# A hybrid diffusion step on one core: up projection in products of 388, 384 and 386 columns, head maxima in two float32r products, transposing mode, a shorter layer-norm sum, and stores moved between queues

## The chip, the core and the metric

The kernel runs on 1 core of one Trainium2 chip. The metric is the device time of one execution in microseconds (us). TensorE does the matrix products into PSUM (8 banks), VectorE and ScalarE do elementwise work, GpSimd and SyncE mainly issue transfers here. Each engine works through its own instructions in order; semaphores join them.

## What is computed

One layer of a diffusion backbone for 128 context tokens and 256 latent tokens (384 in all), width 2048, in float32:

```python
h = rmsnorm(x, norm_mix_pre) * (1 + sc1) + sh1
z = h @ w_in + b_in
glu = z[..., :WA] * sigmoid(z[..., WA:2*WA])
a = along_rows(dwconv(31 taps), glu)
y_a = silu(layernorm(a, ln_a_w, ln_a_b)) @ w_a_out          # layer norm over 512 channels
y_b = einsum(pool_groups(...), w_pool) * pool_scale
hc, new_state = mlstm_bidir(q, k, v, gates, C0, n0, m0)     # 4 heads of 256, two directions
y_c = (hc * rsqrt(mean(hc * hc) + EPS) * mlstm_norm_w * sigmoid(og)) @ w_c_out
mix = (ga * y_a + gb * y_b + gc * y_c) @ w_out
x = x + g1 * rmsnorm(mix, norm_mix_post)
h2 = rmsnorm(x, norm_ffn_pre) * (1 + sc2) + sh2
u, g = split(h2 @ w_ffn_up, 2)                              # 2048 -> 2 x 5632
f = (gelu(dwconv(g, 3 taps)) * u) @ w_ffn_down
x = x + g2 * rmsnorm(f, norm_ffn_post)
```

The mLSTM weights scores by `exp(logd - m_t)`, where `m_t` is a running maximum per head and direction.

## The kernel before

Activations lie transposed, features on the 128 partitions and the 384 tokens along the free dimension, in 16 blocks `hx[k]`. Every float32 operand of a large product is split in two float32r parts: `hi`, a rounded copy by ScalarE, and `lo`, the rest, by VectorE (`split`, L167). A product is then three products into the same PSUM bank (`mm3`, L176): `wh x hi`, `wh x lo`, `wl x hi`, recorded as L177, L178 and L179. In the value projection they are L877 to L879, in the down projection L1490 to L1492.

The weights come as a stream of pieces of 512 KB (24 products each where a tile of 128 output features takes 8 blocks). `run_stream` (L187) writes the order of all engines by hand: for each piece it splits the piece two ahead, issues the piece's products, then the work that evacuates the piece before, and then one entry of each of three background queues `bgq`. Three buffers each hold split weights, so a split waits until TensorE has left the piece three back.

The parts that the change touches:

- Gates and heads. `gate_rows3` (L621) writes the negated running maxima `NM` (36 rows x 512 columns). For each head `head_parts` queues 14 steps; step `s1` multiplies `NM` by a column of the identity repeated 128 times, so that one head's row stands on all partitions (L913, float32), adds the masks (L916), computes the scores, and turns K by two products with the identity (L928). Step `s12` turns the head's output by six products with the identity (L1034), after `s11` has scaled it on VectorE (L1022).
- Layer norm of the convolution branch, `ln_parts` (L707): its 9 steps stand in a background queue beside the heads' steps. `p1` and `p3` sum the four channel tiles, and their squares, over the partitions by four products each with a matrix of ones (L713, L727), in banks 4 to 7 that the heads use too.
- Up projection. The scale of the RMS norm is applied after the product, so the two shift vectors (context and latent) ride along as two extra columns of `hx[k]`: 386 columns instead of 384. `h2_step` (L1309) makes block k+2 while TensorE works on block k of the first six tiles (`up0_use`); the other 82 tiles follow in `up_use`. `up_after` evacuates a pair of tiles.
- End. `down_last` (L1529) finishes the three token blocks of the second half of the output one after another; `down_out` takes the squares (ScalarE, L1524) and evacuates (VectorE, L1526); `down_finish` (L1546) scales four column blocks (VectorE, L1553) and stores each.

Two transpositions elsewhere already use TensorE's transposing mode: the residual, turned by 48 of them (L1451).

```python
            if t:
                down_finish(t - 1)
        down_finish(2)
```

## Time and profile before

| | |
|---|---|
| median of 3 runs | 2293.03 us (2292.72 to 2294.73) |
| the profiled execution | 2294.96 us |
| its span, first to last instruction | 2293.2 us |
| mean granted TensorE clock | 0.993 |
| TensorE busy | 2253.0 us (98%), 12597 products |
| VectorE busy | 1426.8 us (62%) |
| ScalarE busy | 880.8 us (38%) |
| GpSimd busy | 31.7 us (1%) |
| DMA | 390.05 MB, mean 170 GB/s |

The profiled execution's own time is 1.8 us more than its span; what lies around the span is start and end of the program. A busy time adds up durations that overlap in TensorE's pipeline, so a product's price is better read from the distance between the starts of two products than from its duration.

### The profile page before, as it was taken

Reading aid. Unit: us, or ns where it says so; the run is one execution under the profiler, and the core shown is the slowest. Engines: PE = TensorE matmul, PEld = TensorE weight load, DVE = VectorE, ACT = ScalarE, POOL = GpSimd, SP = SyncE. Lnnn points to the kernel's source line nnn. Section 1 sums busy time; section 2 is a strip of 40 time slices with the busy share of each in tenths; the row PEclk is TensorE's granted clock in tenths of the full one; section 3 lists DMA queues with packets and bytes.
Section 4 is the critical chain, followed back from the end, with each engine's and each line's share of the span. In section 5 each row is a group of like instructions: output and inputs, shape, how many; then the busy total and the mean of one; then the engine's idle time right before and its main releaser. Section 6 shows DMA issues by size and latency. Waiting matters only on the chain.

```text
span 2293.2 us, 31786 instructions
## 1 busy us (share of the span) xinstructions
PE 2253.0 (98%) x12597; PEld 2143.6 (93%) x12597; DVE 1426.8 (62%) x2230; ACT 880.8 (38%) x1362; POOL 31.7 (1%) x72
## 2 busy tenths in 40 slices
PE   6999999999999999999999999999999999999997
PEld 3799999999999999999989999999999999888886
DVE  3466777655888888868476577775444445444445
ACT  3443333534232322343366433333333334334332
POOL 0000000000000000000000000000000000000000
PEclk8999999999999999999999999999999999999999
DMA  9944333325666676667433455554433333334342
GB/s 397 392 140 122 122 107 118 120 94 180 221 221 224 232 230 222 223 226 274 146 99 127 135 185 192 180 189 151 140 127 126 122 127 123 131 129 150 129 131 101
DMA packets 104869, 390.05 MB, mean 170 GB/s; under 512 B 12112, under 2 KB 12256, under 8 KB 100624
## 3 DMA queue, kind: packets, MB, share of 16 engines
q1 hardware_dynamic: 99504, 371.76, 47.9%
q0 software_dynamic: 4064, 14.36, 1.9%
q8 instruction: 98, 1.61, 0.3%
q10 hardware_dynamic: 1152, 1.90, 0.2%
q14 instruction: 51, 0.42, 0.1%
HBM read 382.71 MB, written 5.27 MB: 169 GB/s over the span
## 4 chain that ended last, share of the span: by engine, by line
PE 97%; DVE 1%; DMA 1%; ACT 1%; issue 0%; ACTq 0%; DVEq 0%
PE ps L177 24%; PE ps L179 24%; PE ps L178 24%; PE ps L1491 5%; PE ps L1490 5%; PE ps L1492 5%; PE ps L393 1%; PE ps L878 1%; PE ps L879 1%; PE ps L877 1%; DMA eraw<-w_ada 1%; PE ps L974 1%; PE ps L969 1%; PE ps L913 0%; DVE wlo L169 0%; DMA vec<-vec 0%
## 5 line engine op out<-in xcount | busy, mean ns | idle before, releaser
L169 DVE TENSOR_TENSOR wlo<-raw,whi 128x1024 fp32r<-128x1024 f32 (+3 forms) x521 | 622.2, 1197 | 726.9 <-ACT whi L168 724.7
L177 PE MATMUL ps<-hx,whi 128*128 128x384 f32 (+1 forms) x3024 | 1024.8, 339 | 5.6 <-ACT hx L1294 3.2
L179 PE MATMUL ps<-hx,wlo 128*128 128x384 f32 (+1 forms) x3024 | 1019.1, 337 | 0.8 <-DVE wlo L169 0.8
L178 PE MATMUL ps<-hx,whi 128*128 128x384 f32 (+1 forms) x3024 | 1018.9, 337 | 0.2 <-DVE hx L169 0.2
L168 ACT ACTIVATE whi<-raw 128x1024 fp32r<-128x1024 f32 (+3 forms) x521 | 540.0, 1038 | 1231.8 <-PE ps L178 748.2
L177 PEld LDWEIGHTS ps<-hx,whi 128*128 128x128 f32 x3024 | 570.4, 189 | 12.3 <-issue 5.0
L179 PEld LDWEIGHTS ps<-hx,wlo 128*128 128x128 f32 x3024 | 570.1, 189 | 2.0 <-DVE wlo L169 2.0
L178 PEld LDWEIGHTS ps<-hx,whi 128*128 128x128 f32 x3024 | 570.2, 189 | 1.2 <-DVE hx L169 0.5
L1155 DVE SCALAR_TENSOR_TENSOR cb<-raw,cb 128x1024 f32<-128x1024 f32 x256 | 313.0, 1223 | 7.3 <-DMA raw<-w_ada 1.3
L1491 PE MATMUL ps<-whi,hx 128*128 128x512 f32 x528 | 205.5, 389 | 0.8 <-DVE hx L169 0.8
L1490 PE MATMUL ps<-whi,hx 128*128 128x512 f32 x528 | 205.5, 389 | 0.0
L1492 PE MATMUL ps<-wlo,hx 128*128 128x512 f32 x528 | 205.4, 389 | 0.0
L1491 PEld LDWEIGHTS ps<-whi,hx 128*128 128x128 f32 x528 | 99.1, 188 | 21.7 <-DVE hx L169 1.1
L1490 PEld LDWEIGHTS ps<-whi,hx 128*128 128x128 f32 x528 | 99.1, 188 | 20.8 <-ACT hx L168 0.4
L1492 PEld LDWEIGHTS ps<-wlo,hx 128*128 128x128 f32 x528 | 99.1, 188 | 20.7
L692 DVE SCALAR_TENSOR_TENSOR cacc<-cbuf,vec,cacc 128x444 f32<-128x444 f32 x116 | 78.7, 678 | 2.8
L1382 DVE SCALAR_TENSOR_TENSOR t<-t,vec,t 128x192 f32<-128x192 f32 (+1 forms) x176 | 63.7, 383 | 16.0 <-ACT t L1373 12.8
L877 PE MATMUL ps<-whi,hx 128*128 128x256 f32 x192 | 56.5, 294 | 0.0
L878 PE MATMUL ps<-whi,hx 128*128 128x256 f32 x192 | 54.3, 283 | 0.0
L879 PE MATMUL ps<-wlo,hx 128*128 128x256 f32 x192 | 54.3, 283 | 0.0
L393 PE MATMUL ps<-eraw,cs 128*32 128x512 f32 x256 | 34.7, 675 | 18.6 <-DMA eraw<-w_ada 18.6
L169 DVE TENSOR_TENSOR hx<-f,hx 128x384 fp32r<-128x384 f32 x88 | 48.3, 550 | 0.0
(283 smaller groups left out, 1430.6 us busy)
## 6 DMA issues: line engine op xcount, KB each, us to landing
raw<-w_up SPq DMA_DIRECT2D x164, 512.0 KB, 3.6
raw<-w_in SPq DMA_DIRECT2D x163, 512.0 KB, 3.8
raw<-w_ada SPq DMA_DIRECT2D x128, 512.0 KB, 4.3
raw<-w_down SPq DMA_DIRECT2D x88, 512.0 KB, 3.3
eraw<-w_ada SPq DMA_DIRECT2D x32, 1024.0 KB, 17.1
raw<-w_out SPq DMA_DIRECT2D x32, 512.0 KB, 4.3
raw<-w_v SPq DMA_DIRECT2D x16, 512.0 KB, 4.0
raw<-w_br SPq DMA_DIRECT2D x16, 512.0 KB, 4.7
```

Of the source, the lines that this page charges most:

```text
L168: act.activation(hi, src, AF.Copy)
L169: dve.tensor_sub(lo, src, hi.bitcast(F32))
L177: pe.matmul(out, wh, x, start=first, stop=False, skip_group_check=True)
L178: pe.matmul(out, wh, xl, start=False, stop=False, skip_group_check=True)
L179: pe.matmul(out, wl, x, start=False, stop=last, skip_group_check=True)
L692: dve.scalar_tensor_tensor(a, b[:, j : j + CPOS], w, a, ALU.mult, ALU.add)
L877: pe.matmul(outs[t], xh, hi[:, a], start=k == 0 and t != 1, stop=False, skip_group_check=True)
L878: pe.matmul(outs[t], xl, hi[:, a], start=False, stop=False, skip_group_check=True)
L1155: dve.scalar_tensor_tensor(MX["junk"], raw, 1.0, MX["cb"][c][half], ALU.mult, ALU.mult, accum_out=MODR[:, m, n, c, half : half + 1])
L1490: pe.matmul(ps, xh, hi[:, w], start=first, stop=False, skip_group_check=True)
L1491: pe.matmul(ps, xl, hi[:, w], start=False, stop=False, skip_group_check=True)
L1492: pe.matmul(ps, xh, lo[:, w], start=False, stop=last, skip_group_check=True)
```

## The change

In the up projection the shift columns' high and low parts stand side by side in one operand `full`: the first product of a triplet takes 388 columns (tokens, shifts high, shifts low), the second the low part of the tokens alone (384), the third 386. The two sums of shift columns are added later, by VectorE, in `up_after`. The maxima `NM` are split in two float32r parts and multiplied in two products by a float32r copy of 40 columns of the identity, `identr`, which ScalarE makes at the start. K and the head's output are turned in transposing mode. The layer norm adds its four tiles on VectorE and sums by one product each; the second sum's bank is taken from the four banks that the z tiles rotate through, and the steps become 11. `down_finish(t)` is called for each token block right after its products, and all stores go to SyncE's queue but two of the last block. The scratch memory for the descriptors of GpSimd's transfers is halved.

```diff
-HW = NT + 2
+HW = NT + 4
...
+    identr = cp.tile([P, 40], F32R, name="identr")
...
+    act.activation(identr, ident[:, 0:40], AF.Copy)
...
     def gate_rows3():
-        NM = Z["p"].tile([36, 512], F32, name="NM")
         M = Z["M"]
-        gp.memset(NM, 0.0)
-        dve.tensor_scalar_mul(NM[:, 0:LAT], M[:, SEQ:], -1.0)
...
+        NM.hi = Z["p"].tile([36, 512], F32R, name="NMh")
+        NM.lo = Z["p"].tile([36, 512], F32R, name="NMl")
+        gp.memset(NM.hi.bitcast(F32), 0.0)
+        gp.memset(NM.lo.bitcast(F32), 0.0)
...
+            act.activation(NM.hi[rows, dst], M[rows, src], AF.Copy, scale=-1.0)
+            dve.scalar_tensor_tensor(NM.lo[rows, dst], M[rows, src], -1.0, NM.hi[rows, dst].bitcast(F32), ALU.mult,
+                                     ALU.subtract)
...
         def p1():
+            t = tmp()
+            dve.tensor_add(t, glu["d", 0], glu["d", 1])
+            for c in (2, 3):
+                dve.tensor_add(t, t, glu["d", c])
+            L["s"] = t
+
+        def p1b():
             L["ps"] = bgbank()
-            for c in range(4):
-                pe.matmul(L["ps"][:, :NT], ones, glu["d", c], start=c == 0, stop=c == 3)
+            pe.matmul(L["ps"][:, :NT], ones, L["s"], start=True, stop=True)
...
         def p3():
-            L["sq"] = []
-            L["ps"] = bgbank()
+            s = tmp()
             for c in range(4):
-                t = tmp()
-                act.activation(t, glu["d", c], AF.Square)
-                pe.matmul(L["ps"][:, :NT], ones, t, start=c == 0, stop=c == 3)
+                sumsq_tile(s, glu["d", c], c == 0)
+            L["sq"] = s
+
+        def p3b():
+            L["ps"] = accbank()
+            pe.matmul(L["ps"][:, :NT], ones, L["sq"], start=True, stop=True)
...
-        return [p1, p2, p3, p4, p5(0), p5(1), p5(2), p5(3), p5(4)]
+        return [p1, p1b, p2, p3, p3b, p4, p5(0), p5(1), p5(2), p5(3), p5(4)]
...
-                pe.matmul(ps, ident[0:36, r : r + 1].broadcast_to([36, P]), Z["NM"], start=True, stop=False,
-                          skip_group_check=True)
+                one = identr[0:36, r : r + 1].broadcast_to([36, P])
+                pe.matmul(ps, one, Z["NM"].hi, start=True, stop=False, skip_group_check=True)
+                pe.matmul(ps, one, Z["NM"].lo, start=False, stop=False, skip_group_check=True)
...
-                pe.matmul(psy[:, SEQ + c * P : SEQ + (c + 1) * P], k[c][:, 0:SEQ], ident, start=False, stop=True,
-                          skip_group_check=True)
+                pe.transpose(psy[:, SEQ + c * P : SEQ + (c + 1) * P], k[c][:, 0:SEQ], ident)
...
-                    pe.matmul(ps[:, t * P : (t + 1) * P], W["hs"][:, t, c * P : (c + 1) * P], ident, start=t == 0,
-                              stop=True, skip_group_check=True)
+                    pe.transpose(ps[:, t * P : (t + 1) * P], W["hs"][:, t, c * P : (c + 1) * P], ident)
...
     def h2_c(k):
         if k < KD:
-            dve.tensor_sub(hx[k].lo, HU[k], hx[k].hi.bitcast(F32))
+            h = hx[k]
+            h.lo = h.lo[:, :NT]
+            dve.tensor_sub(h.lo, HU[k][:, :NT], h.full[:, :NT].bitcast(F32))
+            dve.tensor_sub(h.full[:, NT + 2 :], HU[k][:, NT:], h.full[:, NT : NT + 2].bitcast(F32))
...
+    def up_mm(ps, wh, wl, x, first, last):
+
+        pe.matmul(ps[:, :HW], wh, x.full, start=first, stop=False, skip_group_check=True)
+        pe.matmul(ps[:, :NT], wh, x.lo, start=False, stop=False, skip_group_check=True)
+        pe.matmul(ps[:, : NT + 2], wl, x.full[:, : NT + 2], start=False, stop=last, skip_group_check=True)
...
-            act.activation(hb[:, 0:2], pu[:, NT:HW], AF.Copy)
-            act.activation(hb[:, 2:4], pg[:, NT:HW], AF.Copy)
+            hb4 = tmp("hb4", 8, bufs=2).rearrange("p (a c) -> p a c", a=2)
+            act.activation(hb4[:, 0], pu[:, NT:HW], AF.Copy)
+            act.activation(hb4[:, 1], pg[:, NT:HW], AF.Copy)
+            dve.tensor_add(hb.rearrange("p (a c) -> p a c", a=2), hb4[:, :, 0:2], hb4[:, :, 2:4])
...
-            if t:
-                down_finish(t - 1)
-        down_finish(2)
+            down_finish(t)
...
-            (sync if n % 2 else act).dma_start(o["y"][t * P : (t + 1) * P, n * NB : (n + 1) * NB], g)
+            (act if t == 2 and n % 2 else sync).dma_start(o["y"][t * P : (t + 1) * P, n * NB : (n + 1) * NB], g)
...
-    nc = bacc.Bacc("TRN2", target_bir_lowering=False, num_devices=1, dynamic_dma_scratch_size=8192)
+    nc = bacc.Bacc("TRN2", target_bir_lowering=False, num_devices=1, dynamic_dma_scratch_size=4096)
```

Where the code is written in another order, the engines' instructions move. First TensorE at the start of the first head (`s1`): before, the float32 product of the maxima of the first direction stands between the stream's products and the masks (`LDWEIGHTS` and `MATMUL` with `identb`).

```order
L179 MATMUL ps_1695<-hx_544,wlo_1621 128x384
L913 MATMUL ps_1727<-NM,ident 128x512
L916 LDWEIGHTS identb
L916 MATMUL ps_1727<-mask,identb 128x128
L916 LDWEIGHTS identb
```

And in the changed kernel:

```order
L180 MATMUL ps_1703<-hx_546,wlo_1629 128x384
L933 MATMUL ps_1735<-NMh,identr 128x512
L934 MATMUL ps_1735<-NMl,identr 128x512
L936 LDWEIGHTS identb
L936 MATMUL ps_1735<-mask,identb 128x128
```

One product has become two in the same place; nothing else in this piece moves, and the transpositions keep their places.

Second, VectorE where the layer norm meets the third head. Before, the layer norm's reciprocal (`sig<-t`) and the scaling of its tiles (`cout`) stand ahead of the head's last unit (`dn`, `hs`), with three weight splits (`wlo`) between them and the final scaling of the head's output (`hss`, L1020).

```order
L169 TENSOR_TENSOR wlo_3714<-raw_3480,whi_3713 128x1024
L733 RECIPROCAL sig_3745<-t_3743 128x384
...
L995 SCALAR_TENSOR_TENSOR hs_3372<-nd_3755,dn_3757,hs_3372 128x256
L169 TENSOR_TENSOR wlo_3763<-raw_3542,whi_3762 128x1024
L842 TENSOR_SCALAR k_3793<-ps_3662,vec 128x384
L745 TENSOR_TENSOR cout_1921<-cout_1921,t_3795 128x384
L169 TENSOR_TENSOR wlo_3814<-raw_3602,whi_3813 128x1024
L745 TENSOR_TENSOR cout_2453<-cout_2453,t_3843 128x384
L169 TENSOR_TENSOR yal_1066<-cout_1921,yah_1065 128x384
L1020 RECIPROCAL hss_3798<-hss_3798 128x3
L1022 TENSOR_SCALAR hs_3372<-hs_3372,hss_3798 128x256 x3
```

And in the changed kernel:

```order
L1014 SCALAR_TENSOR_TENSOR hs_3386<-nd_3756,dn_3758,hs_3386 128x256
L170 TENSOR_TENSOR wlo_3764<-raw_3556,whi_3763 128x1024
L861 TENSOR_SCALAR k_3794<-ps_3671,vec 128x384
L170 TENSOR_TENSOR wlo_3814<-raw_3615,whi_3813 128x1024
L752 RECIPROCAL sig_3845<-t_3843 128x384
L755 TENSOR_TENSOR cout_1931<-cout_1931,sig_3845 128x384
L756 TENSOR_SCALAR cout_1931<-cout_1931,vec 128x384
...
L756 TENSOR_SCALAR cout_3532<-cout_3532,vec 128x384
L1039 RECIPROCAL hss_3798<-hss_3798 128x3
L1041 TENSOR_SCALAR hs_3386<-hs_3386,hss_3798 128x256 x3
L170 TENSOR_TENSOR wlo_3873<-raw_3669,whi_3872 128x1024
```

The layer norm's reciprocal and its eight scalings now stand between the last weight split and the scaling of the head's output, which the transpositions of step `s12` read.

Third, VectorE at the end of the program. Before, the four scalings of token block 1 (`fo_18055` to `fo_19250`) stand behind both evacuations of block 2 (`fo_19274`, `fo_19290`).

```order
L1526 TENSOR_TENSOR fo_19274<-ps_18090,gb_18075 128x512
...
L1526 TENSOR_TENSOR fo_19290<-ps_18091,gb_18075 128x512
L1550 RECIPROCAL r_19292<-r_19292 128x1
L1553 SCALAR_TENSOR_TENSOR fo_18055<-fo_18055,r_19292,x_9047 128x512
...
L1553 SCALAR_TENSOR_TENSOR fo_19250<-fo_19250,r_19292,x_9047 128x512
L1550 RECIPROCAL r_19303<-r_19303 128x1
L1553 SCALAR_TENSOR_TENSOR fo_18069<-fo_18069,r_19303,x_9047 128x512
```

In the changed kernel they stand ahead of them (`fo_18176` to `fo_19382` is block 1, `fo_19406` and `fo_19422` block 2):

```order
L1578 RECIPROCAL r_19384<-r_19384 128x1
L1581 SCALAR_TENSOR_TENSOR fo_18176<-fo_18176,r_19384,x_9064 128x512
...
L1581 SCALAR_TENSOR_TENSOR fo_19382<-fo_19382,r_19384,x_9064 128x512
L1556 TENSOR_TENSOR fo_19406<-ps_18211,gb_18196 128x512
...
L1556 TENSOR_TENSOR fo_19422<-ps_18212,gb_18196 128x512
L1578 RECIPROCAL r_19424<-r_19424 128x1
L1581 SCALAR_TENSOR_TENSOR fo_18190<-fo_18190,r_19424,x_9064 128x512
```

Each block is scaled right behind its own evacuations. ScalarE's row of the end loses four of its six stores.

## Rows read from the trace of the kernel before

**Rows 1.** The page: the busy time of the engines (part 1), and the chain that ended last, by line (part 4).
```profile
PE 2253.0 (98%) x12597; PEld 2143.6 (93%) x12597; DVE 1426.8 (62%) x2230; ACT 880.8 (38%) x1362; POOL 31.7 (1%) x72
PE ps L177 24%; PE ps L179 24%; PE ps L178 24%; PE ps L1491 5%; PE ps L1490 5%; PE ps L1492 5%; PE ps L393 1%; PE ps L878 1%; PE ps L879 1%; PE ps L877 1%; DMA eraw<-w_ada 1%; PE ps L974 1%; PE ps L969 1%; PE ps L913 0%; DVE wlo L169 0%; DMA vec<-vec 0%
```

**Rows 2.** Busy time in stretches of the span: start and end, length, then busy us and instructions of TensorE, its weight loads, VectorE, ScalarE and GpSimd, the granted TensorE clock (1.00 is the upper level), the busy share of the DMA engines, GB/s. The heads, the restart ahead of the up projection, the up projection, the turning of the residual.
```profile
172.00:400.00 228.00, 228.00 (x1410) 218.94 (x1409) 167.75 (x306) 79.01 (x118) 7.50 (x17) 1.00 0.38 118
1156.00:1170.00 14.00, 9.06 (x39) 8.16 (x39) 7.85 (x15) 7.87 (x21) 0.00 (x0) 0.76 0.16 54
1228.00:1896.00 668.00, 668.00 (x3802) 667.79 (x3801) 397.29 (x623) 262.35 (x426) 1.60 (x3) 1.00 0.46 151
1270.00:1310.00 40.00, 40.00 (x247) 39.87 (x246) 20.54 (x32) 18.62 (x32) 0.00 (x0) 1.00 0.40 131
```

**Rows 3.** Timeline of TensorE: start us, duration us, engine, line, operation and its tiles, shape, count. First and 31st of a run of products with 384 columns, first and 31st of one with 386, first and 43rd of one with 512.
```profile
800.38 0.33 PE L177 MATMUL ps<-hch,whi 128*128 128x384 f32 x1
...
805.58 0.33 PE L177 MATMUL ps<-hx,whi 128*128 128x384 f32 x1
...
1500.08 0.34 PE L178 MATMUL ps<-hx,whi 128*128 128x386 f32 x1
...
1505.38 0.34 PE L178 MATMUL ps<-hx,whi 128*128 128x386 f32 x1
...
2271.50 0.39 PE L1492 MATMUL ps<-wlo,hx 128*128 128x512 f32 x1
...
2281.02 0.39 PE L1492 MATMUL ps<-wlo,hx 128*128 128x512 f32 x1
```

**Rows 4.** Timeline of TensorE at the start of the first head. Two float32 records make one float32 product.
```profile
200.12 0.34 PE L179 MATMUL ps<-hx,wlo 128*128 128x384 f32 x1
200.39 1.12 PE L913 MATMUL ps<-NM,ident 36*128 36x512 f32 x2
201.44 0.34 PE L916 MATMUL ps<-mask,identb 128*128 128x128 bf16 x3
...
205.17 0.61 PE L928 MATMUL ps<-ident,k 128*128 128x128 f32 x4
205.54 0.42 PE L177 MATMUL ps<-hx,whi 128*128 128x384 f32 x1
```

**Rows 5.** The chain that ended last, in order of time: start us, length us, what. A head's six products against the identity (12 records), and 12 transpositions of the residual (12 records).
```profile
265.02 1.34 PE ps L1034 x12
...
1275.41 1.31 PE ps L1451 x12
```

**Rows 6.** The same chain where the last pooling tile is followed by the branch products.
```profile
526.55 1.24 DVE wlo L169
527.84 0.44 PE ps L179
```

**Rows 7.** The same chain at the two sums of the layer norm (8 records each).
```profile
401.09 2.59 PE ps L713 x8
...
414.28 2.58 PE ps L727 x8
```

**Rows 8.** Timeline of VectorE at the layer norm's scaling and at the third head's output scaling, and the chain at that head's transpositions.
```profile
418.85 2.55 DVE L733 RECIPROCAL sig<-t 128x384 f32<-128x384 f32 x1 [2.40 <-ACT t L731]
...
425.37 0.15 DVE L988 SCALAR_TENSOR_TENSOR dn<-nd 128x1 f32<-128x1 f32 x1
...
431.53 0.88 DVE L1022 TENSOR_SCALAR hs<-hs,hss 128x256 f32<-128x256 f32 x3
...
435.72 1.34 PE ps L1034 x12
```

**Rows 9.** Timeline at the first products of the up projection, and VectorE in two later steps of it; in brackets the idle time ahead of an instruction and what ended it.
```profile
1164.59 0.69 PE L177 MATMUL ps<-hx,whi 128*128 128x386 f32 x1 [3.24 <-ACT hx L1294]
1165.18 0.69 PE L178 MATMUL ps<-hx,whi 128*128 128x386 f32 x1
...
1180.82 0.96 DVE L169 TENSOR_TENSOR wlo<-raw,whi 128x768 fp32r<-128x768 f32 x1 [0.22 <-ACT whi L168]
...
1184.00 0.96 DVE L169 TENSOR_TENSOR wlo<-raw,whi 128x768 fp32r<-128x768 f32 x1 [0.22 <-ACT whi L168]
```

**Rows 10.** Timeline at the end of the program: VectorE, and ScalarE's queue of stores (ACTq).
```profile
2271.97 0.69 DVE L1526 TENSOR_TENSOR fo<-ps,gb 128x512 f32<-128x512 f32 x1 [1.54 <-ACT junk L1524]
2272.57 0.15 DVE L1539 TENSOR_TENSOR sp<-ss 128x1 f32<-128x1 f32 x1
...
2278.95 2.74 DVE L1553 SCALAR_TENSOR_TENSOR fo<-fo,r,x 128x512 f32<-128x512 f32 x4
2279.73 1.68 ACTq L1554 DMA_DIRECT2D y<-fo  x2
...
2284.07 2.74 DVE L1553 SCALAR_TENSOR_TENSOR fo<-fo,r,x 128x512 f32<-128x512 f32 x4
...
2287.09 2.74 DVE L1553 SCALAR_TENSOR_TENSOR fo<-fo,r,x 128x512 f32<-128x512 f32 x4
```

**Rows 11.** Timeline at the start of the program, and the list of transfers issued there: size, median us from issue to landing.
```profile
1.25 0.70 POOL L288 DMA_DIRECT2D ident<-ident  x1 [0.81 <-POOLq L1671]
...
15.34 1.93 PE L393 MATMUL ps<-eraw,cs 128*32 128x512 f32 x8 [15.34 <-DMA eraw<-w_ada]
...
ident<-ident POOLq DMA_DIRECT2D x1, 64.0 KB, 6.3
```

More of the change, by code (lines that the diff above doesn't have):

```diff
@@ L621, in gate_rows3 @@
     def gate_rows3():
-        NM = Z["p"].tile([36, 512], F32, name="NM")
         M = Z["M"]
-        gp.memset(NM, 0.0)
-        dve.tensor_scalar_mul(NM[:, 0:LAT], M[:, SEQ:], -1.0)
-        dve.tensor_scalar_mul(NM[0:4, LAT : LAT + P], M[0:4, SEQ + P :], -1.0)
-        dve.tensor_scalar_mul(NM[32:36, LAT : LAT + P], M[32:36, SEQ : SEQ + P], -1.0)
-        dve.tensor_scalar_mul(NM[:, LAT + P :], M[:, 0:SEQ], -1.0)
+        NM = Two()
+        NM.hi = Z["p"].tile([36, 512], F32R, name="NMh")
+        NM.lo = Z["p"].tile([36, 512], F32R, name="NMl")
+        gp.memset(NM.hi.bitcast(F32), 0.0)
+        gp.memset(NM.lo.bitcast(F32), 0.0)
+        for rows, dst, src in (
+            (slice(0, 36), slice(0, LAT), slice(SEQ, NT)),
+            (slice(0, 4), slice(LAT, LAT + P), slice(SEQ + P, NT)),
+            (slice(32, 36), slice(LAT, LAT + P), slice(SEQ, SEQ + P)),
+            (slice(0, 36), slice(LAT + P, 512), slice(0, SEQ)),
+        ):
+            act.activation(NM.hi[rows, dst], M[rows, src], AF.Copy, scale=-1.0)
+            dve.scalar_tensor_tensor(NM.lo[rows, dst], M[rows, src], -1.0, NM.hi[rows, dst].bitcast(F32), ALU.mult,
+                                     ALU.subtract)
         Z["NM"] = NM
@@ L1289, in h2_b @@
             x = X["x"][:, k]
-            u = tmp("sig", HW, bufs=3)
+            u = tmp("sig", NT + 2, bufs=3)
             scaled(u, x, S2, k)
@@ L1293, in h2_b @@
             pr = h_pair(f"hx{k}", HW)
-            act.activation(pr.hi, u, AF.Copy)
+            pr.full = pr.hi
+            act.activation(pr.full[:, : NT + 2], u, AF.Copy)
             hx[k] = pr
@@ L1338, in f @@
                 w = slice(c * P, (c + 1) * P)
-                mm3(acc["up", c][:, :HW], hi[:, w], lo[:, w], hx[k].hi, hx[k].lo, k == 0, k == KD - 1)
+                up_mm(acc["up", c], hi[:, w], lo[:, w], hx[k], k == 0, k == KD - 1)
             h2_step(k + 2)
@@ L1403, in f @@
                 k = 8 * part + a
-                mm3(acc["up", t][:, :HW], hi[:, a], lo[:, a], hx[k].hi, hx[k].lo, k == 0, k == KD - 1)
+                up_mm(acc["up", t], hi[:, a], lo[:, a], hx[k], k == 0, k == KD - 1)
         return f
```

## The prediction

> **What bounds the kernel now.** I read the page's chain first: it runs through TensorE's three product lines L177 to L179, and TensorE has work for 98% of the span [rows 1]. Then the stages: in the heads, in the up projection and in the stretch with the transpositions TensorE is busy from end to end at full clock [rows 2], while VectorE has 167.75 of 228 us and 397.29 of 668 us. So what is taken off TensorE in these stages comes off the span, and work given to VectorE or ScalarE is free while it stays inside their gaps. Two stretches are different: around 1156 to 1170 us TensorE stops and comes back at half clock [rows 2], and after its last product the end belongs to ScalarE, VectorE and the stores.
>
> **The sum.** The profiled execution took 2294.96 us with a span of 2293.2; it lies 1.93 above the median of the runs, 2293.03. The terms are differences and are taken from the median.
>
> *Up projection.* A product's price is its start-to-start pitch, since durations overlap. 30 products of 384 columns take 5.20 us, 173.3 ns each; 30 of 386 take 5.30 us, 176.7 ns; 42 of 512 take 9.52 us, 226.7 ns [rows 3]. From 384 to 512 a column costs 0.417 ns, so 386 should cost 174.2; it costs what that slope gives for 392. Two extra columns are therefore paid as eight. The change makes each triplet 388, 384 and 386 columns: the sum of columns is unchanged (1158), but only two of three products pass 384. If 388 lies on the step of 386, a triplet falls from 530.0 to 526.7 ns, and 1408 triplets (the count of 386-column products on L177 is 1408: 88 tiles by 16 blocks of features) give -4.7 us. The bounds: 0 if the price grows evenly beyond 384 (the 388-column product then costs 180.0), -7.0 if 388 is free of the penalty (175.0). I take -4.7, since one step for both is the simplest reading.
>
> The Trainium skill, "TensorE: Matmul & The Clock Gate", section Back-to-back issue gap, gives a product as its columns divided by the clock plus a constant. By that rule the triplet costs the same before and after, and the edit is worth 0 instead of -4.7. The trace disagrees with it at 386 columns (176.7 ns, where the rule's slope from 384 gives 174.2).
>
> *Head maxima.* The float32 product with 512 columns holds TensorE from 200.39 to 201.44 us, 1.05 [rows 4]; there are 8 (two a head). Two float32r products of 512 columns cost 2 x 0.227 = 0.453. That is -0.60 each, -4.8; entering and leaving may cost or give up to 0.2 each (the step into it at 200.12 to 200.39 is 0.27 where 0.17 is normal). I take -4.6, bounds -3.2 to -5.6.
>
> *Transposing mode.* Six float32 products against the identity take 1.34 us as 12 records; 12 products already in transposing mode take 1.31 us [rows 5]. So a transposition is one record where the product is two, and six cost 0.66: -0.68 in each of four heads, -2.7. The two of K cost 0.37 (205.17 to 205.54) [rows 4] and would cost 0.22: four times -0.15, -0.6. The last head's six stand some 10 us ahead of a place where TensorE waits for VectorE's weight split (526.55 to 527.84) [rows 6], whose chain does not start from them, so about 0.7 is waited away again: -2.6 in all, bounds -1.9 to -3.4.
>
> The Trainium skill, same page, Part 4: PE-mode transpose, says that transposing mode does not count as work for the clock gate. No fall of the clock shows here: the stretch with 48 transpositions in four bursts has clock 1.00 [rows 2].
>
> *Layer norm.* Each of the two sums is four float32 products, 2.59 and 2.58 us [rows 7]; one is left of each: -3/4 of 5.17 = -3.9, bounds -3.3 to -4.2. The six additions and the squares lie in VectorE's and ScalarE's gaps. But the chain has two steps more, so the reciprocal and eight operations on the four channel tiles now stand on VectorE just ahead of the third head's final scaling of its output, whose transpositions wait for it. Before, the reciprocal and the eight took 418.85 to 425.37, 6.5 us, and the scaling started at 431.53, 4.2 us ahead of TensorE's 435.72 [rows 8]. After, TensorE is there at 435.72 - 3.9 = 431.8. The second sum's product now stands a little over two pieces of 24 products (4.16 us each) ahead of these transpositions and is done at about 421.7; the reciprocal starts some 2 us behind it, when ScalarE has split a piece, changed its table and taken the root: 423.7, plus 6.5 is 430.2, plus 1.1 for the scaling 431.3. Half a microsecond of slack is left of 4.2, on an estimated start. I put +0.2 (0 to 1).
>
> *First block of the up projection.* The low part of the two shift columns is now made by VectorE after its 384-column subtraction and read by the first product. Before, that product started at 1164.59 when ScalarE was done, and the second at 1165.18 after the subtraction [rows 9]. Now the first waits for subtraction and tail, to about 1165.25, and the second follows at half clock: +0.5 (0.2 to 1). For later blocks the operands are two blocks ahead. There VectorE waits 0.22 us in each step of 3.18 [rows 9]; a tiny operation takes 0.15 [rows 10] and a pitch of 0.19, so it fits with almost nothing over. If it didn't, 14 steps of some 0.1 us would be absorbed by the two blocks of lead: 0.
>
> *Hidden.* The 40 columns copied at the start hold ScalarE, and behind it the sigmoid and VectorE's product that TensorE's first instruction needs, until the identity lands: issued at 1.25, 6.3 us, so 7.6; TensorE starts at 15.34 when its weights land [rows 11]. Nearly 8 us of cover; later than about 13 us it would cost one for one. The 44 additions of shifts (0.19 each) and the split maxima sit in VectorE's idle 40%. Halved descriptor memory adds no wait that I can see: GpSimd issues at most four transfers in a row. The shifted z banks are reused with one other tile between, no reader is late: 0.
>
> *The end.* Before, ScalarE issues two stores of the first token block (1.68 us from 2279.73) ahead of the last block's squares; and VectorE runs eight scalings after the last product (2281.02 [rows 3]): four from 2284.07 and four from 2287.09, 2.74 each time, ending 2289.83 [rows 10]. After, token block 0 is scaled between the products of block 1. VectorE's work for a block is two evacuations, three tiny sums, a reciprocal and four scalings: 0.6 + 0.57 + 0.6 + 0.19 + 2.74 = 4.7. From the first block's end at about 2277.7 (the second evacuation starts nine products of 0.227 behind 2271.97, at 2274.0; plus 0.69, the reciprocal's 0.19 and 2.74) two blocks more give 2287.1 to 2287.5 against 2289.83: -2.5, bounds -1.5 to -3.3. ScalarE has no store ahead of the last squares; the stores of the last block alternate as before, and the landing behind the last scaling (3.4 us to the end of the span) is kept.
>
> Sum: -4.7 - 4.6 - 2.6 - 3.9 - 2.5 + 0.2 + 0.5 = -17.6. 2293.03 - 17.6 = **2275.4 us**.
>
> **The rivals.**
> 1. *The up edit does nothing* (price even in columns): 2275.4 + 4.7 = 2280.1. For it: equal sums. Against: the step at 386 [rows 3]. 13%. Its mirror, 388 without penalty, 2273.1: 11%.
> 2. *Slower: 388 columns fall on the next larger step.* Place: the first of each triplet. The nearest larger row is 512 columns, 226.7 ns: +50 ns over the forecast's, times 1408 = +70 us, about 2346. It decides from a pitch of 192 ns on: the other terms give 12.9, 0.2% is 4.6, 17.5/1408 = 12.4 ns over today's triplet. Against: past 384 the step was 3.3 ns only. 4%.
> 3. *The clock falls at the transpositions*, as the restart at 1164.59 shows it: clock 0.76 over 14 us [rows 2], that is 3.4 us lost. Eight bursts with 2.3 to 3.4 lost each, 18 to 27 us, would eat everything: about 2294 to 2302. Against stands the clock of 1.00 in the four longer bursts [rows 2]. 4%. The rule that speaks for it is the one cited above from the Trainium skill, "TensorE: Matmul & The Clock Gate", Part 4: PE-mode transpose.
> 4. *Late chains*: the third head's scaling misses by several us, or tile reuse around the moved layer norm makes TensorE wait; 5 to 9 us come back: 2281 to 2284. For it: the half microsecond of slack counted above. 8%.
> The forecast itself: 60%.
>
> **The numbers.** A change of 0.2% (4.6 us) is about what a measurement of this kernel can tell from none. Faster holds the forecast, both sides of rival 1, and rival 4: 0.60 + 0.24 + 0.08 = 0.92. Rival 3 falls half within 0.2% (0.02) and half beyond it (0.02); with rival 2, slower has 0.06. The range for 8 in 10 runs from the mirror of rival 1 less a microsecond (stronger gains at maxima and end) to just past rival 1: 2271.5 to 2281.0.
>
> **What would show it.** Pitches of the triplet of 176.7, 173.3, 176.7 ns at 388, 384, 386 columns. The maxima's pair at 0.45 to 0.5 us. Six transpositions in 0.66. One float32 sum of 0.65 in place of each of the two. The last scaling ending 6.1 to 6.5 us behind the last product's start, where it was 8.8. TensorE's wait at the first block of the up projection longer by half a microsecond, and one short or no wait ahead of the third head's transpositions. The prediction is wrong if the triplet's sum stays at 530 ns or grows, if the clock falls behind the bursts, or if TensorE's idle time grows by more than 2 us.

## The result, and the profile after

The kernel after takes 2276.39 us (median; 2275.46 to 2277.23), the kernel before, run beside it, 2293.07: a ratio of 0.9924, 95% interval 0.9912 to 0.9935, or -16.7 us. The profiled execution took 2277.23 with a span of 2275.4, against 2294.96 and 2293.2 before, so the two traces differ by 17.8.

The page of after: busy time of the engines, and the groups of the three products of the up projection (count, busy us, mean ns, idle time ahead and what ended it).

```profile
PE 2237.1 (98%) x12553; PEld 2132.7 (94%) x12553; DVE 1434.6 (63%) x2296; ACT 881.6 (39%) x1366; POOL 32.1 (1%) x73
L1357 PE MATMUL ps<-hx,whi 128*128 128x388 f32 x1408 | 481.5, 342 | 4.0 <-DVE hx L1327 4.0
L1359 PE MATMUL ps<-hx,wlo 128*128 128x386 f32 x1408 | 476.6, 339 | 0.0
L1358 PE MATMUL ps<-hx,whi 128*128 128x384 f32 x1408 | 472.4, 336 | 0.0
```

TensorE is still the bound, with 16 us less to do than in [rows 1]; VectorE and ScalarE carry the added work inside their gaps. Stretches of after, columns as in [rows 2]: the restart, the up projection, the turning of the residual.

```profile
1146.00:1160.00 14.00, 8.30 (x39) 7.74 (x38) 8.07 (x18) 7.88 (x21) 0.00 (x0) 0.76 0.17 54
1220.00:1888.00 668.00, 668.00 (x3825) 667.78 (x3825) 401.61 (x664) 263.38 (x427) 1.60 (x3) 1.00 0.46 152
1259.00:1300.00 41.00, 41.00 (x253) 40.85 (x252) 20.70 (x34) 19.13 (x33) 0.00 (x0) 1.00 0.40 130
```

In 668 us of the up projection 3825 products run where 3802 ran before, at the same full clock. Timeline of TensorE in after: the first product of a triplet and that of the tenth triplet behind it, and the first head's maxima (answers to [rows 3, 4]):

```profile
1480.13 0.34 PE L1357 MATMUL ps<-hx,whi 128*128 128x388 f32 x1
...
1485.39 0.34 PE L1357 MATMUL ps<-hx,whi 128*128 128x388 f32 x1
...
200.41 0.34 PE L180 MATMUL ps<-hx,wlo 128*128 128x384 f32 x1
200.68 0.49 PE L933 MATMUL ps<-NMh,identr 36*128 36x512 f32 x1
201.01 0.39 PE L934 MATMUL ps<-NMl,identr 36*128 36x512 f32 x1
201.34 0.34 PE L936 MATMUL ps<-mask,identb 128*128 128x128 bf16 x3
```

Ten triplets (three products each) take 5.26 us, 526.7 ns each over 1216 triplets of the trace (530.0 before). A direction's maxima, from the start of the last projection product to the mask, take 0.93 us where [rows 4] has 1.32; but the two products hold 0.66, not 0.45.

The chain of after, in order of time, at six transpositions and at the two layer-norm sums (answers to [rows 5, 7]); and the timeline at the first block of the up projection and at the end ([rows 9, 10]).

```profile
264.37 0.66 PE ps L1053 x6
...
402.72 0.65 PE ps L730 x2
...
416.75 0.65 PE ps L746 x2
```

```profile
1150.48 0.93 PE L319 MATMUL ps<-ident,rc 128*128 128x128 f32 x6 [0.56 <-DVE rc L317]
...
1154.64 0.56 DVE L1326 TENSOR_TENSOR hx<-sig,hx 128x384 fp32r<-128x384 f32 x1 [0.46 <-ACT hx L1313]
1155.12 0.15 DVE L1327 TENSOR_TENSOR hx<-sig,hx 128x2 fp32r<-128x2 f32 x1
1155.42 0.67 PE L1357 MATMUL ps<-hx,whi 128*128 128x388 f32 x1 [4.00 <-DVE hx L1327]
...
2266.50 0.39 PE L1522 MATMUL ps<-wlo,hx 128*128 128x512 f32 x1
...
2269.33 2.74 DVE L1581 SCALAR_TENSOR_TENSOR fo<-fo,r,x 128x512 f32<-128x512 f32 x4
```

The wait ahead of the first block has grown from 3.24 to 4.00 us, and the last scaling ends 5.57 us behind the last product's start (2272.07 less 2266.50), where it was 8.81.

### The profile page after: what moved, and what is told of

The parts are those of the page before. It is cut to its first block, busy times and chain, and to the rows that moved or that the text cites. A ratio compares the mean times of both kernels' runs of the same rounds, so it can differ in the third digit from the quotient of the medians.

```text
span 2275.4 us, 31790 instructions
## 1 busy us (share of the span) xinstructions
PE 2237.1 (98%) x12553; PEld 2132.7 (94%) x12553; DVE 1434.6 (63%) x2296; ACT 881.6 (39%) x1366; POOL 32.1 (1%) x73
## 4 chain that ended last, share of the span: by engine, by line
PE 96%; DVE 2%; DMA 1%; ACT 1%; issue 1%; DVEq 0%; POOL 0%; SPq 0%; ACTq 0%
PE ps L178 13%; PE ps L180 13%; PE ps L179 13%; PE ps L1357 11%; PE ps L1359 11%; PE ps L1358 11%; PE ps L1521 5%; PE ps L1522 5%; PE ps L1520 5%; PE ps L396 1%; PE ps L898 1%; PE ps L897 1%; PE ps L896 1%; DMA eraw<-w_ada 1%; PE ps L993 1%; PE ps L988 1%
## 5 line engine op out<-in xcount | busy, mean ns | idle before, releaser
L178 PE MATMUL ps<-hx,whi 128*128 128x384 f32 x1616 | 546.7, 338 | 2.5 <-ACT whi L169 2.5
L180 PE MATMUL ps<-hx,wlo 128*128 128x384 f32 x1616 | 541.6, 335 | 1.4 <-DVE wlo L170 1.4
L179 PE MATMUL ps<-hx,whi 128*128 128x384 f32 x1616 | 541.4, 335 | 0.2 <-DVE hx L170 0.2
L1357 PE MATMUL ps<-hx,whi 128*128 128x388 f32 x1408 | 481.5, 342 | 4.0 <-DVE hx L1327 4.0
L1359 PE MATMUL ps<-hx,wlo 128*128 128x386 f32 x1408 | 476.6, 339 | 0.0
L1358 PE MATMUL ps<-hx,whi 128*128 128x384 f32 x1408 | 472.4, 336 | 0.0
```

The costliest lines, as they stand in the source:

```text
L178: pe.matmul(out, wh, x, start=first, stop=False, skip_group_check=True)
L179: pe.matmul(out, wh, xl, start=False, stop=False, skip_group_check=True)
L180: pe.matmul(out, wl, x, start=False, stop=last, skip_group_check=True)
L1357: pe.matmul(ps[:, :HW], wh, x.full, start=first, stop=False, skip_group_check=True)
L1358: pe.matmul(ps[:, :NT], wh, x.lo, start=False, stop=False, skip_group_check=True)
L1359: pe.matmul(ps[:, : NT + 2], wl, x.full[:, : NT + 2], start=False, stop=last, skip_group_check=True)
```

## The experiments

**The up projection's edit alone.** The kernel before, with only the diff's parts on the up projection (`h2_b`, `h2_c`, `up_mm`, the sums of the shifts).

> The kernel before with the up projection's edit alone: 388, 384 and 386 columns, the two additions of the shifts, and the low part of the shifts made by VectorE behind the subtraction. Theory (columns beyond 384 are paid by a step that 386 and 388 share): ten triplets in 5.26 us instead of 5.30, 1408 triplets give -4.7 to -5.6 us; the stop ahead of the first block grows by about 0.75 us; ratio 0.9980 to 0.9985. Rival (the price grows evenly with the columns, and after's shorter triplet came from another edit): 5.30 us, no gain, and with the longer stop a ratio of 1.0003.

Measured: 2290.33 against 2294.20, ratio 0.9983 (0.9974 to 0.9992), -3.9 us; 526.7 ns over 1232 triplets. Ten of them:

```profile
1494.49 0.34 PE L1339 MATMUL ps<-hx,whi 128*128 128x388 f32 x1
...
1499.75 0.34 PE L1339 MATMUL ps<-hx,whi 128*128 128x388 f32 x1
```

The gain is this edit's own, and rival 1 of the prediction falls. But the reading behind it, a step that 386 and 388 share, is not yet tested by this.

**Two columns fewer in the third product.**

```diff
-        pe.matmul(ps[:, : NT + 2], wl, x.full[:, : NT + 2], start=False, stop=last, ...)
+        pe.matmul(ps[:, :NT], wl, x.full[:, :NT], start=False, stop=last, ...)
```

> The kernel after, with 384 instead of 386 columns in the third product of each triplet of the up projection: it leaves out the low part of the weights times the two shift columns. Theory (386 lies on the step above 384): 1408 times 3.3 ns, 4.7 us less than after, about 2271.7 us or a ratio of 0.9903 to the kernel before. Rival (the price is even, 0.417 ns a column): 1408 times 0.8 ns, 1.2 us less, a ratio of 0.9918.

Measured: 2281.10, ratio 0.9944 (0.9930 to 0.9957): some 4.6 us slower than after. Both theories fail in sign. The timeline, first products ten triplets apart:

```profile
1480.38 0.34 PE L1357 MATMUL ps<-hx,whi 128*128 128x388 f32 x1
...
1485.68 0.34 PE L1357 MATMUL ps<-hx,whi 128*128 128x388 f32 x1
```

530 ns again: 388, 384 and 384 columns cost what three times 386 did, and more than 388, 384, 386. TensorE has no wait there in either kernel. A product of 384 columns thus has no fixed price of its own.

**Other widths, one product at a time.** In 72 of the 88 tiles the first or the third product takes another width:

```diff
+        pe.matmul(ps[:, :w1], wh, x.full[:, :w1], start=first, stop=False, ...)
         pe.matmul(ps[:, :NT], wh, x.lo, start=False, stop=False, ...)
+        pe.matmul(ps[:, :w3], wl, x.full[:, :w3], start=False, stop=last, ...)
```

> The kernel after, with other widths in 72 of the 88 tiles of the up projection: in 36 of them the first product of the triplet takes 388, 390, 392, 394, 396, 398, 400, 404, 408, 412, 416 or 424 columns in turn, in 36 others the third takes 352, 360, 364, 368, 372, 376, 378, 380, 382, 384, 386 or 388. It leaves out the columns that a narrower product does not reach; a wider one adds zeros. Theory A (price in steps of eight columns, 3.3 ns each): 388, 390 and 392 the same, 394 to 400 3.3 ns more, 404 and 408 again 3.3 more, 412 and 416 again, 424 again, and downward 378, 380, 382 and 384 the same, 372 and 376 3.3 ns less, 368 6.7 less, 360 10 less, 352 13.3 less. Theory B (even price of 0.417 ns a column with one fixed addition as soon as 384 is passed): 392 costs 1.7 more than 388, 400 5.0 more, 416 11.7 more, and below 384 an even slope, 380 lower by 1.7 and 382 by 0.8. Theory C (what counts is whether the columns divide by 4 or by 8, not how many): 388 or 392 on the slope from 384, with 386, 390, 394 and 398 dearer than their neighbours on both sides.

Measured, mean of 30 to 48 triplets, from start to start of the first product, in ns. Third product, after 388 and 384: 352 508, 360 516, 364 to 378 520, **380 514**, 382 520, 384 529, 386 527, 388 527. First product, ahead of 384 and 386: 390 527, **392 532**, 394 527, 396 531, 398 527, 400 to 408 533 to 534, 412 to 424 539 to 541. The dip at 380 is no noise of the reading. Ten triplets with 380 columns in the third product, and ten with 384:

```profile
1595.63 0.34 PE L1361 MATMUL ps<-hx,whi 128*128 128x388 f32 x1
...
1600.77 0.34 PE L1361 MATMUL ps<-hx,whi 128*128 128x388 f32 x1
...
1612.17 0.34 PE L1361 MATMUL ps<-hx,whi 128*128 128x388 f32 x1
...
1617.45 0.34 PE L1361 MATMUL ps<-hx,whi 128*128 128x388 f32 x1
```

With 380 columns ten triplets take 5.14, with 384 5.28: 14 ns a triplet for four columns, where the slope of [rows 3] gives 1.7. Theory A (steps of eight), B (even price) and C (divisibility) all fail: the time goes up and down with the width, in jumps.

**Forms of the triplet.** 32 forms in two tiles each: a table of widths, and for eight of them the low weights second.

> The kernel after, with 32 forms of the triplet in 64 of the 88 tiles of the up projection, two tiles each. In 24 forms the order is as after (high weights times high part, high weights times low part, low weights times high part), in 8 the low weights stand second. Twelve of the 24 narrow a product to 384 or 386 columns and leave out some of the shift columns' parts; the others only add zeros. Theory 1 (each product has its own price, whatever stands beside it): with the widths in program order, 384/384/384 takes 520.0 ns, each 386 or 388 adds 3.3, so 386/384/384, 384/386/384 and 384/384/386 523.3, every two of them 526.7, every three 530.0, and 388/384/384 523.3. Theory 2 (a triplet is paid as a whole: 13.3 ns a product and 0.417 a column is the floor, 520.0 for three of 384 and 522.5 for a sum of 1158, and what comes above it depends on which widths follow each other): 388/384/384 again 530, the three places of a single 386 differ from one another by 3.3 or more, and among the forms with sums of 1158 and 1160 some take 522 to 524 and others 530, order of the weights included.

Measured (28 triplets or a few fewer each), in ns: 384/384/384 521; 386/384/384 520, 384/386/384 521, 384/384/386 521; 386/384/386 524, 386/386/384 525; 386/386/386 530; 388/384/382 520; 388/386/384 530; 388/384/386 527; **388/386/386 522**; 388/386/388 526; 388/388/388 530; 390/384/384 533, 392/384/384 526; 390/386/386 and 392/386/386 533. With the low weights second: 388/386/384 530, 388/386/386 522, 388/386/388 526, 388/388/386 529. The eleven forms not listed lie between 526 and 533. Theory 1 is refuted at once: the first 386 costs nothing, the third costs 5, and two more columns in the last place of 388/386/384 take 8 ns away. Of Theory 2 the first half stands, a triplet is paid as a whole; that the place of a single 386 decides does not (all 520 or 521). Ten triplets of 388/386/384 and of 388/386/386, order as after, with the fourth of the latter between:

```profile
1349.73 0.34 PE L1401 MATMUL ps<-hx,whi 128*128 128x388 f32 x1
...
1355.03 0.34 PE L1401 MATMUL ps<-hx,whi 128*128 128x388 f32 x1
...
1450.98 0.34 PE L1401 MATMUL ps<-hx,whi 128*128 128x388 f32 x1
...
1452.57 0.33 PE L1401 MATMUL ps<-hx,whi 128*128 128x388 f32 x1
...
1456.21 0.33 PE L1401 MATMUL ps<-hx,whi 128*128 128x388 f32 x1
```

Read one by one, the triplets show what these means hide: after about three triplets a tile settles into a pattern that repeats. In the tile of 388/386/386 shown, the first three take 1.59 us (535, 530 and 524 ns) and the seven behind them 3.64, 520 each. So 522 is a mean over slow starts, and the settled triplet takes 520. The others are patterns too: 386/384/386 takes 520 and 527 in turn, 386/386/386 528 and 532, 388/386/384 527 and 533. And the widths alone do not fix the pattern: 388/388/386 with the low weights second settled at 531 in one tile and at 527 in the other.

**Two columns of zeros more, everywhere.**

```diff
+            gp.memset(pr.lo[:, NT : NT + 2].bitcast(F32), 0.0)
+            pr.lox = pr.lo[:, : NT + 2]
...
-        pe.matmul(ps[:, :NT], wh, x.lo, start=False, stop=False, ...)
+        pe.matmul(ps[:, : NT + 2], wh, x.lox, start=False, stop=False, ...)
```

> The kernel after with 386 instead of 384 columns in the second product of every triplet of the up projection; the two added columns of the low part are zeros, written by GpSimd. Theory 2 (a triplet is paid as a whole, and 388/386/386 was read at 522.1 ns in two tiles of either order, against 526.7 for 388/384/386): ten triplets take 5.22 us, 1408 times 4.6 ns are 6.5 us, about 2269.9 us, a ratio of 0.9896 to the kernel before. Theory 1 (each product has its own price, and 386 costs 3.3 ns more than 384): 530 ns, 4.7 us more than after, 2281 us, 0.9947. Third possibility (the 522.1 belonged to those tiles' neighbours and not to the widths): 526.7 and no change, 0.9927.

Measured: 2267.47, ratio 0.9885 (0.9871 to 0.9900), some 9 us less than after, more than Theory 2 gave. The triplet takes 520.1 ns (1312 triplets), as three products of 384 do in the projections, though it has 8 columns more:

```profile
1480.07 0.33 PE L1359 MATMUL ps<-hx,whi 128*128 128x388 f32 x1
...
1485.27 0.33 PE L1359 MATMUL ps<-hx,whi 128*128 128x388 f32 x1
```

1408 times 6.6 ns is 9.3 us. 520.1 also lies below Theory 2's floor (523.3 for 1160 columns): that floor is wrong too. That the gain is larger than Theory 2's 6.5 us follows from the 522.1 it was taken from, which held the slow starts of two tiles; here all tiles have the same widths, and the slow start (535, 530, 524) comes once, behind the restart. What sets the rhythm stays open; shown is only that it depends on the three widths together and not on their sum, and in one form also on how the tile began.

**The maxima's rows.** Heads 1 and 3 contract 128 rows, and the second direction reads a stored tile:

```diff
+                n = P if h % 2 else 36
+                one = identr[0:n, r : r + 1].broadcast_to([n, P]) if d == 0 else Z["REP"][0:n, h]
+                pe.matmul(ps, one, Z["NM"].hi[0:n], start=True, ...)
+                pe.matmul(ps, one, Z["NM"].lo[0:n], start=False, ...)
```

> The kernel after, with four forms of the maxima's two products: heads 0 and 2 contract 36 rows, heads 1 and 3 all 128 rows (zeros in the added ones); the first direction reads the one column repeated by its address as before, the second a stored tile of 128 equal columns. After, a direction's two products and the step into the mask take 0.66 us, and the step from the projection into the first product 0.27 where 0.17 is normal. Theory A (weights of 36 rows are not loaded ahead of weights of 128 rows, nor the other way round): in heads 1 and 3 the two products take 0.45 to 0.50 us and the step into them 0.17, in both directions; heads 0 and 2 stay at 0.66 and 0.27. Theory B (the repeated column is slow to load): the second direction falls to 0.45 to 0.50 in all four heads, the first stays at 0.66. Theory C (the price lies in the switch to another tensor's bank or to the bfloat16 mask): all eight stay at 0.6 to 0.7.

Timeline of TensorE in the second head, and of its weight loads (PEld) in the first and the second:

```profile
279.82 0.34 PE L180 MATMUL ps<-hx,wlo 128*128 128x384 f32 x1
280.00 0.40 PE L938 MATMUL ps<-NMh,identr 128*128 128x512 f32 x1
280.23 0.40 PE L939 MATMUL ps<-NMl,identr 128*128 128x512 f32 x1
280.47 0.34 PE L941 MATMUL ps<-mask,identb 128*128 128x128 bf16 x3
...
199.17 0.18 PEld L938 LDWEIGHTS ps<-NMh,identr 36*128 36x128 f32 x1 [0.25 <-issue]
...
279.83 0.19 PEld L938 LDWEIGHTS ps<-NMh,identr 128*128 128x128 f32 x1
```

With 128 rows the step in takes 0.18 and the two products 0.47; in heads 0 and 2, 0.26 to 0.27 and 0.66 to 0.67, for either source. With 36 rows the first product's weights are loaded only when the product itself starts (199.17, behind 0.25 idle); with 128 rows while the product before still runs (279.83, ahead of 280.00). That is shown for the first product alone: the second one's weights are loaded 0.22 ahead of it in the first head too (199.28 for 199.50), and yet it takes 0.33 to the mask there and 0.24 with 128 rows. Why is open. Theory A holds in the first direction; in the second, behind the mask, 0.55 is left. The stored tile brings nothing (with the repeated address the last kernels below show 0.56 there), so Theory B falls. From the last projection product to the scores a head takes 1.53 instead of 2.03: 0.5 us a head. (One execution, 2274.20 us; its start is 1.5 us earlier by chance, see the next run.)

**The small waits.**

```diff
-            dve.tensor_sub(h.lo, HU[k][:, :NT], h.full[:, :NT].bitcast(F32))
             dve.tensor_sub(h.full[:, NT + 2 :], HU[k][:, NT:], h.full[:, NT : NT + 2].bitcast(F32))
+            dve.tensor_sub(h.lo, HU[k][:, :NT], h.full[:, :NT].bitcast(F32))
```

and the 40 columns copied in `gate_rows3`.

> The kernel after, with two moves: the 40 columns are copied just ahead of the first use, at the gates' rows, instead of at the start; and in the first block of the up projection VectorE makes the low part of the two shift columns ahead of the 384-column subtraction instead of behind it. Theory: the 0.25 us that TensorE's projections lie behind the kernel before from 178 us on come back, and of the 0.75 us by which the restart at the first block is later some 0.3 to 0.5; 0.5 to 0.8 us less than after in all, a ratio of 0.9920 to 0.9923 to the kernel before. Rival (the copy is hidden, the start's 0.25 is that execution's own, and the first block waits for the subtraction in either order): the matching starts stay at +0.25 and +0.75, 0 us.

Measured: 2276.05, ratio 0.9921 (0.9907 to 0.9934): no difference from after that can be told. The timeline at the first block:

```profile
1149.85 1.65 PE L317 MATMUL ps<-ident,rc 128*128 128x128 f32 x6 [0.56 <-DVE rc L315]
...
1154.73 0.16 DVE L1325 TENSOR_TENSOR hx<-sig,hx 128x2 fp32r<-128x2 f32 x1 [0.46 <-ACT hx L1312]
...
1154.94 0.69 PE L1356 MATMUL ps<-hx,whi 128*128 128x388 f32 x1 [3.44 <-DVE hx L1325]
```

The wait is 3.44 instead of 4.00, as the theory has it; but in this execution six products ahead of it took 1.65 us where after's took 0.93, so the clock had fallen earlier (to half at 1149.46, ahead of these products; in after at 1152.72, behind them), and the gain is gone. Of the start the rival holds: without the early copy the first head's maxima start at 200.64, with it at 200.68 in after, and at 198.97 to 200.36 in eight other kernels of this study that have it. The 0.25 us was the execution's own.

**The layer norm's bank.**

```diff
-            L["ps"] = accbank()
+            L["ps"] = bgbank()
```

> The kernel after, with the layer norm's second sum in a bank of the background rotation, as the first, instead of a z bank. Theory (the gain of the layer norm is the six products fewer, 4.25 us between the matching starts around it, and the bank only decides which tile it must wait for): from 395.9 to 435.7 of the kernel before, the same stretch stays within 0.3 us of after's. Rival (the background banks are held by late readers at that place): TensorE waits there, and 0.5 to 4 us of the 4.25 are lost.

Measured: 2279.68 (one execution). The waits of TensorE between 385 and 460 us, of which after has none:

```profile
PE ps L1033 <- ACT t L750: 2.2, 1, 2.2
```

The rival holds. The third head's state products (L1033) take the four banks that this rotation goes through, and wait for the layer norm's root (L750), which still reads the sum. By this trace the z bank is worth 2.2 of the layer norm's 4.3 us.

**The end, in its two parts.** First the order of the scalings as before, then the stores' queues as before.

```diff
-            down_finish(t)
+            if t:
+                down_finish(t - 1)
+        down_finish(2)
```

> The kernel after, with the order at the end as in the kernel before (the first token block's results are scaled behind the products of the second, the last two behind the last product) and the stores' queues as after. After, the last scaling ends 5.57 us behind the last product's start, before 8.8. Theory (the end is set by how many scalings VectorE has left behind the last product, eight instead of four and a bit): 8.3 to 8.8 us, the whole of the end's gain gone. Rival (the gain came from the stores leaving ScalarE's queue): 5.6 to 6.2 us.

```diff
-            (act if t == 2 and n % 2 else sync).dma_start(o["y"]...
+            (sync if n % 2 else act).dma_start(o["y"]...
```

> The kernel after, with the stores' queues as in the kernel before (every second one from ScalarE) and the order of the scalings as after. Theory (VectorE's count of scalings sets the end): the last scaling still ends 5.6 to 6.0 us behind the last product's start. Rival (two stores of the second token block, 1.68 us on ScalarE's queue, stand ahead of the last block's square and its root): the root and all behind it come 1 to 2 us later, 6.6 to 7.6 us.

Timeline at the end, of the first kernel and of the second (one execution each, 2278.55 and 2277.67 us):

```profile
2265.39 0.39 PE L1522 MATMUL ps<-wlo,hx 128*128 128x512 f32 x1
...
2270.65 2.74 DVE L1583 SCALAR_TENSOR_TENSOR fo<-fo,r,x 128x512 f32<-128x512 f32 x4
```

```profile
2265.81 0.39 PE L1522 MATMUL ps<-wlo,hx 128*128 128x512 f32 x1
...
2267.21 0.60 ACT L1554 ACTIVATE junk<-ps 128x512 f32<-128x512 f32 x1 [2.81 <-DVE fo L1581]
...
2269.78 2.74 DVE L1581 SCALAR_TENSOR_TENSOR fo<-fo,r,x 128x512 f32<-128x512 f32 x4
```

The last scaling ends 8.00 us behind the last product's start with the old order and 6.71 with the old queues, 5.57 in after. Both parts work: 2.4 us for the order, 1.1 for the queues. The first rival falls, but 8.00 lies below that theory's 8.3 too, so the order is not the whole of the end's gain; of the second run the rival holds, since the last block's first square (2267.21) now waits for the scalings whose results ScalarE has to store.

**The points that paid, together.** First 128 rows in all maxima, the order and the copy of the small waits, and two of the three small sums of each block made earlier; then the zeros as well.

```diff
+                one = identr[:, r : r + 1].broadcast_to([P, P])
...
+                    dve.scalar_tensor_tensor(sp, ss4[:, t, 2:3], 1.0 / D, sp, ALU.mult, ALU.add)
```

> The kernel after with four moves: the maxima's products contract 128 rows in both directions and all heads (zeros in the added ones); the first block's shift columns are made ahead of the subtraction; the 40 columns are copied at the gates' rows; and at the end two of the three one-column sums a block on VectorE are made earlier, when the first half of the columns is done. Expected against after: maxima -0.5 us a head, -2.0; first block -0.6; end -0.4 for each block of which VectorE sets the pace, -0.8 to -1.1: 3.4 to 3.7 less, about 2272.8 us, a ratio of 0.9905 to 0.9908 to the kernel before. Rival (the end is set by the root of the last block and the stores, not by VectorE's pace): -2.6 us, 0.9912.

Measured: 2273.02, ratio 0.9909 (0.9892 to 0.9925). By its time the run can't tell the theory from its rival (0.9912). The rows speak for the theory: 1.36 us from the maxima to the scores instead of 1.77, and the last scaling ends 4.81 us behind the last product's start (2268.06 less 2263.25) instead of 5.57, and at the first block the wait is 3.44 with the six products ahead of it at 0.93 again.

> The kernel with 128 rows in the maxima's products, the first block's shift columns ahead of the subtraction, the 40 columns copied at the gates' rows and the earlier sums at the end, and with the second product's 386 columns added. By Theory 2: 6.5 us less than without them, 2266.5 us, a ratio of 0.9880. By Theory 1: 2277.7, 0.9929.

Measured: 2264.78, ratio 0.9874 (0.9858 to 0.9890) to the kernel before; 520.1 ns a triplet. Theory 2's side, and 1.7 us better than it gave. This is the fastest version of the study: 28.8 us less than before, 11.6 less than after by the medians.

## Why the prediction was right

The time (2275.4 forecast, 2276.39 measured) lies 1 us off, and the mechanism holds: what was taken off TensorE came off the span. But two terms, the head maxima and the layer norm, lie just outside their bounds, and the up projection's is right for a reason that is wrong. That it came out to the microsecond is partly luck. The up projection, the maxima's rows, the layer norm's bank and the two parts of the end were each changed alone, the first block and the start together; the terms of the transpositions and of the layer norm's sums are read from the two traces only.

- *Up projection*, -4.7: 1408 times 3.3 ns is 4.6 in the trace, -3.9 (-6.0 to -1.8) timed alone. The step that failed is the price list behind it: "Two extra columns are therefore paid as eight" and "one step for both". With 386 beside 384 two columns cost nothing, and 388/384/384 costs 530. Nor does the rule of the Trainium skill cited in the prediction ("TensorE: Matmul & The Clock Gate", Back-to-back issue gap) hold here: it gives all sums of 1158 columns one price, and 386/386/386, 388/384/386 and 388/386/384 were read at 530, 527 and 530. That section gives the rule for a product taken singly, and says that in a stream of weight loads and products both set the spacing; the prediction asked more of it than it states.
- *Head maxima*, -4.6: 1.32 to 0.93 us, eight times, is -3.1, just outside the bounds. The mis-sized term is the product's 0.227, taken from products of 128 rows; with 36 rows it was 0.33. For the first of each pair the weights came late; for the second the cause is open.
- *Transposing mode*, -2.6: 0.66 for six, as said, in three heads 2.0; K 0.14 instead of 0.37 (204.68 to 204.82), 0.9 in all; -2.9. The last head's 0.7 was waited away as said: ahead of it TensorE's starts moved from 489.26 to 479.30, 9.96 us, and at the wait behind it from 527.84 to 517.87, 9.97; TensorE comes there earlier and waits longer (first line below). The reason given, a chain "whose chain does not start from them", needs a second look, since the view of before has the transpositions right ahead of ScalarE's split at 519.10. What ScalarE waited for there was a buffer: its copies of the head's state go on when the stores of the two before them land (at 518.32 for the copy at 518.42; in after at 508.74 for the one at 508.84, second line). So the reading holds. The clock stays at 1.00 in the bursts, so rival 3 falls.
- *Layer norm*, -3.9 + 0.2: the two sums fall by 1.94 and 1.93; matching starts from 395.91 to 425.64 of before draw together by 4.26. Most of the rest is a wait that went too: in before ScalarE's reading of the first sum stands in the chain ahead of a product of the head (third line below). The transpositions of the third head wait for nothing, but it was close: the scaling ahead of them ends at 427.22 and they start at 427.30 (last two lines), where the prediction counted half a microsecond. The sentence "no reader is late: 0" was right, but the bank was no detail: without it 2.2 us are lost.
- *First block*, +0.5: the wait grew by 0.76. In this execution the stretch at half clock behind it was shorter (3.99 us instead of 5.26), which gave 0.64 back.
- *Hidden start*, 0: right, the 0.25 to 0.3 seen in the trace came with the execution.
- *End*, -2.5: -3.24. VectorE's block took 4.49 us instead of 4.7, and ScalarE's freed queue, not counted by itself, is worth 1.1.

```profile
517.87 0.45 PE L180 MATMUL ps<-hx,wlo 128*128 128x384 f32 x1 [0.65 <-DVE wlo L170]
...
508.84 0.39 ACT L1045 ACTIVATE so<-ps 128x257 f32<-128x257 f32 x1 [0.28 <-DMA cn_out<-so]
...
403.70 0.50 ACT t L717
...
426.32 0.90 DVE L1041 TENSOR_SCALAR hs<-hs,hss 128x256 f32<-128x256 f32 x3
...
427.30 0.82 PE L1053 MATMUL ps<-ident,hs 128*128 128x128 f32 x6
```

The first two and the last two lines are of after (timeline), the third is of before (chain).

-4.6 - 3.1 - 2.9 - 4.26 + 0.76 - 0.64 + 0.27 - 3.24 = -17.7, against 17.8 between the two spans. The maxima missed by +1.5; the end (-0.7), the layer norm (-0.6), the restart (-0.4) and the transpositions (-0.3) made up for it, which is why the sum came out. The stated range is a little wider below than its reason: the mirror of rival 1 less a microsecond is 2272.1, not 2271.5.

## What to carry to other kernels

Where one product follows another without a wait, try the widths of the whole repeated group on the chip, padding included: here two columns of zeros took 9 us off, and leaving two out added 5. Take a product's price from a row with the same number of rows as well as of columns, and pad a short contraction where its weights would come late. An edit that makes a chain shorter is only worth what its bank, its queue and its order leave of it; take each back by itself before calling it a detail.

## What was not expected of the hardware

- Triplets of float32r products at full clock took 520.1 ns with 388/386/386 columns, 526.7 with 388/384/386, 530.0 with 388/384/384 and with 386/386/386: more columns in less time, without a wait in the trace. Each form settles after about three triplets into a pattern of its own (520 throughout, or 528 and 532 in turn). The cause is open.
- Two products of 512 columns took 0.12 to 0.19 us more with 36 rows than with 128, and the step into them from a projection 0.1 more. The first one's weights were loaded only when it started; the second's were not late, and its share is unexplained.
- The granted clock falls at a moment of its own in the stop ahead of the up projection: it went to half at 1152.72 us in after and at 1149.46 in another execution with the same start of the heads, where the same six products took 1.65 us instead of 0.93, so a wait shortened there by half a microsecond does not show in the time.
